# A state space stage cut into small pieces and its output units moved behind the last keys

## The chip, the cores and the metric

The kernel runs on one core of a Trainium2 chip. The metric is the device time of one execution in microseconds. Five engines matter: TensorE (PE in the profile; its weight loads are PEld), VectorE (DVE), ScalarE (ACT), GpSimd (POOL) and SyncE (SP), which issues DMAs. Each engine works through its own list of instructions strictly in order.

## The reference, cut to what matters

512 tokens of width 1024 pass through one block of a first kind and then through four layers of a second kind. The change touches the first block alone:

```
h = rmsnorm(x, norm_mix_g)
proj = h @ w_in                       # u (512 wide), q, k, v (512 each)
y_ssm = s5_mixer(u, ...)              # state space stage
y_att = chunked_attention(q, k, v, rel_bias)
mixed = concat(rmsnorm(y_ssm), rmsnorm(y_att))
x = x + mixed @ w_out
x = x + (silu(h2 @ w_gate) * (h2 @ w_up)) @ w_down    # h2 = rmsnorm(x)

# s5_mixer: 32 groups of 16 channels, 64 complex states per group
lam_bar = exp(lam * exp(log_dt))
b_bar   = ((lam_bar - 1) / lam) * b
state_t = lam_bar * state_{t-1} + b_bar @ u_t
y_t     = real(c @ state_t) + d_skip * u_t
y = gelu(y);  y = y * sigmoid(y @ w_glu + b_glu)
```

The attention has 8 heads of 64 channels; a token sees its own chunk of 64 tokens and the 8 chunks ahead of it. The four later layers also attend to a memory of 256 tokens, whose keys and values (`mem_n @ w_kv`) this kernel computes early, inside the first block's stretch.

## The kernel before

**Products.** Every large product is made in fp32 as three matmuls of a high and a low part (`mm`, L174; lines L185, L187, L189). A weight tile's high part is made by a ScalarE copy (L233), its low part by a VectorE subtraction (L235). The plan is a list of units; a unit is one output tile over four k-tiles, 12 matmuls of 128x512. I call these the main matmuls and count them from the start; those of the memory are 128x256.

**Order.** `execute` (L123) emits the units one after the other. Side work is written as generators. After each main matmul `tick(self.fine)` takes every generator of one list a step further, after each unit `tick(self.gens)` those of the other; `finish(g)` (L204) runs a generator to its end at once. `wait(n)` passes n ticks. A scheduler then moves instructions a little by readiness, and from there every engine's list is fixed.

**The first block before.** Main matmuls 0 to 96 are the four tiles of u. Their norm is gathered (L336) when `squares` (L1509) calls `finish` after the first 48. 96 to 480 are the memory's keys and values for four layers. 480 to 696 are q, k and v for head pairs 0 to 2, 696 to 744 the four output units of the state space stage (`ssm_units`, L1486; they read yh, yl, and SSM_AT = 3 puts them there), 744 to 816 q, k and v of pair 3, 816 to 1008 the two halves of w_out. Then the feed-forward part begins.

**The state space stage before.** `s5_tables` (L1100) makes powers of lam_bar and the matrices of b_bar in many small VectorE operations. `s5_u` (L1249) copies a tile of u out of PSUM, scales it by the norm's factors `bc` (L1257) and writes it to DRAM. `s5_main` (L1322) starts when the tables are done. It loads u per chunk of 8 tokens, makes the chunks' states by 64 small matmuls (S), and spawns `s5_toeps` (L1288), which makes the powers F of the output matrices (`s5_powers`, L1265: 12 operations of 288 elements per quarter m, L1278 to L1283), multiplies them into the kernels within a chunk (L1305), writes these to DRAM and reads them back as Toeplitz matrices `toep`. The recurrence over chunks is 14 steps of three dependent GpSimd operations: L1357 (product, 512 elements), L1358 (sum of the pair, 256), L1359 (added to S, 256). Then come four output stages, m = 0 to 3: S2 is copied out of S (L1370, GpSimd), 16 matmuls S,F (L1376) and 16 matmuls U,toep (L1384) go into one PSUM bank, the result y is copied to a buffer s5x (L1392) and sent to DRAM. F has two buffers, so F of m = 2 and 3 is made after the stages 0 and 1 have read theirs. `s5_gelu` (L1404) reads y back turned, applies gelu (L1415), and splits it into yh, yl.

**Attention.** `qkv_post` (L1572) scales q and makes keys (L1432), then spawns `chunk_pair` (L1437): scores, row maximum and exp (L788), scaling of the probabilities (L1451), transposes, and the product with v (L1469).

## Time and profile before

| | us |
|---|---|
| median of 3 runs (3158.51 to 3159.5) | 3159.09 |
| the profiled execution, its own time | 3160.28 |
| its span | 3158.5 |
| TensorE busy in the span | 3085.0 (98%) |
| VectorE busy | 1773.8 (56%) |
| ScalarE busy | 1362.7 (43%) |
| GpSimd busy | 561.1 (18%) |

TensorE is busy almost throughout, so the average says little. The page's strip of 40 slices shows where it is not: in the first four slices, of 79 us each, its digits are 7, 8, 9, 9, and VectorE's are 9, 9, 8, 7, while in most of the rest VectorE stands at 3 to 5. The first block takes about the first fifth of the span, and the stages that the change touches end where the feed-forward part begins, at 333.42 us. What matters is therefore read by stretches of that part. In the views below, a stretch is given in us from the span's start; PEclk is the granted TensorE clock as a share of full speed; L185, L187 and L189 on xh, xl or yh, yl are main matmuls.

### The profile page before, as it was taken

The numbers are of one execution on the slowest core, as the hardware profiler recorded it, in microseconds if no ns is written. First come the engines' busy times: TensorE is split into PE (matmuls) and PEld (weight loads), VectorE is DVE, ScalarE is ACT, GpSimd is POOL, SyncE is SP. The second block draws the span as 40 slices with busy tenths as digits, with TensorE's granted clock in tenths as the row PEclk, the third lists the DMA queues.
The fourth block names the chain that finished last, engine by engine and source line by source line (L and its number), as shares of the span: only waits on it lengthen the run. The fifth ranks groups of instructions, "written<-read, shape, count | busy, mean of one in ns | idle before, by whom it ended". The sixth has DMA issues, their size and how long they took to land.

```text
span 3158.5 us, 38988 instructions
## 1 busy us (share of the span) xinstructions
PE 3085.0 (98%) x14568; PEld 2576.1 (82%) x14568; DVE 1773.8 (56%) x2995; ACT 1362.7 (43%) x2504; POOL 561.1 (18%) x464
## 2 busy tenths in 40 slices
PE   7898999999999999999999999999999999999998
PEld 6687788888888888888888888887888888878886
DVE  9987644458755344467753445655444477553444
ACT  5366423347754232455432334334333477542332
POOL 2731201032212010111110001112000122120103
PEclk9899999999999999999999999999999999999999
DMA  6332233332223333322233333233333322233332
GB/s 211 110 99 87 85 96 97 98 94 68 69 73 104 100 91 103 94 77 84 67 103 98 92 103 91 86 102 99 96 96 98 98 67 67 62 106 97 94 101 77
DMA packets 101694, 295.28 MB, mean 93 GB/s; under 512 B 22496, under 2 KB 26592, under 8 KB 101472
## 3 DMA queue, kind: packets, MB, share of 16 engines
q1 hardware_dynamic: 101504, 292.79, 31.7%
q8 instruction: 114, 1.87, 0.2%
q14 instruction: 76, 0.62, 0.1%
HBM read 286.20 MB, written 6.55 MB: 93 GB/s over the span
## 4 chain that ended last, share of the span: by engine, by line
PE 91%; DVE 5%; ACT 1%; issue 1%; DMA 1%; POOL 0%; DVEq 0%; SPq 0%; ACTq 0%; POOLq 0%
PE g L185 27%; PE g L189 27%; PE g L187 27%; DVE lo L235 1%; PE a L225 1%; PE a L224 1%; PE z L740 1%; PE a L223 1%; PE z L753 1%; PE a L657 0%; PE a L646 0%; DVE x L427 0%; PE z L189 0%; PE z L185 0%; PE z L187 0%
## 5 line engine op out<-in xcount | busy, mean ns | idle before, releaser
L233 ACT ACTIVATE hi<-raw 128x512 fp32r<-128x512 f32 (+2 forms) x1094 | 662.2, 607 | 1419.3 <-PE g L187 1309.2
L235 DVE TENSOR_TENSOR lo<-raw,hi 128x512 fp32r<-128x512 f32 (+2 forms) x1094 | 765.3, 701 | 656.9 <-ACT hi L233 633.1
L185 PE MATMUL g<-xh,hi 128*128 128x512 f32 x2720 | 1066.6, 392 | 11.5 <-ACT hi L233 7.4
L189 PE MATMUL g<-xh,lo 128*128 128x512 f32 x2720 | 1064.0, 391 | 0.0
L187 PE MATMUL g<-xl,hi 128*128 128x512 f32 x2720 | 1062.6, 391 | 0.0
L185 PEld LDWEIGHTS g<-xh,hi 128*128 128x128 f32 x2720 | 513.0, 189 | 118.7 <-ACT hi L233 7.4
L189 PEld LDWEIGHTS g<-xh,lo 128*128 128x128 f32 x2720 | 512.3, 188 | 105.5 <-DVE lo L235 0.2
L187 PEld LDWEIGHTS g<-xl,hi 128*128 128x128 f32 x2720 | 512.7, 188 | 103.3
L189 PE MATMUL g<-ah,lo 128*128 128x512 f32 x1110 | 433.7, 391 | 3.0 <-DVE lo L235 2.8
L185 PE MATMUL g<-ah,hi 128*128 128x512 f32 x1110 | 432.2, 389 | 2.0 <-ACT t L284 2.0
L187 PE MATMUL g<-al,hi 128*128 128x512 f32 x1110 | 432.1, 389 | 0.0
L440 POOL TENSOR_TENSOR t<-t,bc 128x512 f32<-128x512 f32 x110 | 143.2, 1302 | 1407.3 <-ACT t L439 1407.3
L189 PEld LDWEIGHTS g<-ah,lo 128*128 128x128 f32 x1110 | 208.4, 188 | 50.7 <-DVE lo L235 7.8
L185 PEld LDWEIGHTS g<-ah,hi 128*128 128x128 f32 x1110 | 208.4, 188 | 45.3 <-ACT t L284 2.8
L187 PEld LDWEIGHTS g<-al,hi 128*128 128x128 f32 x1110 | 208.4, 188 | 43.1
L411 DVE TENSOR_TENSOR t<-g,bc 128x512 f32<-128x512 f32 x182 | 124.9, 688 | 169.2 <-PE g L189 164.0
L427 DVE TENSOR_TENSOR x<-x,g 128x512 f32<-128x512 f32 x151 | 103.3, 685 | 133.8 <-PE g L189 133.8
L442 DVE TENSOR_TENSOR t<-g,t 128x512 f32<-128x512 f32 x110 | 76.1, 692 | 180.4 <-PE g L189 160.6
L285 POOL TENSOR_TENSOR acc<-acc,t 128x512 f32<-128x512 f32 x82 | 114.9, 1405 | 329.9 <-ACT t L284 303.7
L233 ACT ACTIVATE ah<-t 128x512 fp32r<-128x512 f32 x110 | 69.5, 632 | 45.4 <-DVE t L442 45.4
L439 ACT ACTIVATE t<-t 128x512 f32<-128x512 f32 x110 | 69.7, 634 | 33.4 <-DVE t L411 33.3
L235 DVE TENSOR_TENSOR al<-t,ah 128x512 fp32r<-128x512 f32 x110 | 76.1, 692 | 11.9 <-ACT ah L233 2.3
(351 smaller groups left out, 3033.1 us busy)
## 6 DMA issues: line engine op xcount, KB each, us to landing
raw<-in_weights_dram SPq DMA_DIRECT2D x436, 512.0 KB, 3.6
raw<-in_weights_dram SPq DMA_DIRECT2D x76, 448.0 KB, 3.4
raw<-in_weights_dram SPq DMA_DIRECT2D x18, 384.0 KB, 3.2
x<-in_xT_dram SPq DMA_DIRECT2D x16, 256.0 KB, 3.7
x<-in_att_bias_dram SPq DMA_DIRECT2D x8, 256.0 KB, 6.2
kv<-kv SPq DMA_DIRECT2D x32, 64.0 KB, 2.4
out_dram<-x SPq DMA_DIRECT2D x8, 256.0 KB, 2.3
mraw<-in_memT_dram SPq DMA_DIRECT2D x2, 512.0 KB, 6.3
```

The source lines that it names most:

```text
L185: nc.tensor.matmul(out=out, lhsT=wh, rhs=xh, start=u.first and i == 0, stop=False)
L187: nc.tensor.matmul(out=out, lhsT=wh, rhs=xl, start=False, stop=False)
L189: nc.tensor.matmul(out=out, lhsT=wl, rhs=xh, start=False, stop=u.last and i == len(u.ks) - 1)
L223: nc.tensor.matmul(out=out, lhsT=ah, rhs=bh, start=start, stop=False)
L233: nc.scalar.activation(out=hi, in_=src, func=ACTF.Copy)
L235: eng.tensor_tensor(out=lo, in0=src, in1=hi.bitcast(F32), op=ALU.subtract)
L285: nc.gpsimd.tensor_tensor(out=norm["acc"][rows, :n], in0=norm["acc"][rows, :n], in1=sq[rows, :n], op=ALU.add)
L411: nc.vector.tensor_tensor(out=t, in0=ps, in1=bc, op=ALU.mult)
L427: self.nc.vector.tensor_tensor(out=self.x[m], in0=self.x[m], in1=ps, op=ALU.add)
L439: nc.scalar.activation(out=tg, in_=tg, func=ACTF.Silu)
L440: nc.gpsimd.tensor_tensor(out=tg, in0=tg, in1=self.bc(n), op=ALU.mult)
L442: nc.vector.tensor_tensor(out=h, in0=ps, in1=tg, op=ALU.mult)
```

## The change

- The tables are cut into small pieces, with a `yield` after every few operations, and `finish` on the first norm goes. `s5_u` copies u out of PSUM at once, into a free tile of x, and waits as a generator until `bc` is there before it scales and stores ("u scaled late").
- `s5_powers` makes F of a quarter in 6 operations of 576 elements, all on VectorE, 6 ticks apart (S5_PACE).
- A new generator `s5_kernels` makes F and the kernels within a chunk before `s5_main` starts. `s5_toeps` only clears the matrices, on GpSimd now, and reads the kernels from DRAM; it stands after the state matmuls.
- `s5_main` waits until all four tiles of u and the kernels are done. The recurrence's 42 operations move from GpSimd to VectorE.
- F for m = 2 and 3 is made after y of m = 0 and 1 has been sent off.
- The four output units move from ahead of q3 to between k3 and v3, and with them `ssm_begin`, which finishes `s5_main`. The attention of a pair waits for its v.

```diff
@@ -52,12 +52,11 @@
-S5_STEP = 10
-S5_FILL = (24, 0)
-S5_POOL = (False, True)
-S5_WAIT = 100
+S5_STEP = 14
+S5_FILL = 8
+S5_PACE = 6
+S5_WAIT = 4
-SSM_AT = 3
...
+        def cmul(out_r, out_i, xr, xi, yr, yi, t, eng, pace=False):
             eng.tensor_tensor(out=out_r, in0=xr, in1=yr, op=mul)
             eng.tensor_tensor(out=t, in0=xi, in1=yi, op=mul)
+            if pace:
+                yield
...
-            cmul(pw[:, 0, :, lo + 1:lo + 1 + w], pw[:, 1, :, lo + 1:lo + 1 + w],
-                 pw[:, 0, :, 1:1 + w], pw[:, 1, :, 1:1 + w], b[0], b[1], t[:, :, :w], V)
+            yield from cmul(pw[:, 0, :, lo + 1:lo + 1 + w], pw[:, 1, :, lo + 1:lo + 1 + w],
+                            pw[:, 0, :, 1:1 + w], pw[:, 1, :, 1:1 + w], b[0], b[1], t[:, :, :w], V)
+            yield
         bb = tail[:, :512].rearrange("p (c a b) -> p c a b", c=2, a=16)
-        cmul(bb[:, 0], bb[:, 1], br, bi, w3[0], w3[1], t, V)
+        yield from cmul(bb[:, 0], bb[:, 1], br, bi, w3[0], w3[1], t, V, True)
+        yield
+        V.tensor_scalar(out=ci, in0=ci, scalar1=-1.0, scalar2=None, op0=mul)
...
@@ -1249,11 +1269,14 @@
     def s5_u(self, m, ps, norm):
-        t = self.tmp()
+
+        t = self.x[4 + m]
         turned = t.rearrange("p (t c) -> p c t", t=8)
         src = ps.rearrange("p (c t) -> p c t", t=8)
 
         nc.scalar.activation(out=turned, in_=src, func=ACTF.Copy)
+        while norm["bc"] is None:
+            yield
         nc.vector.tensor_tensor(
...
-    def s5_powers(self, m, split=(False, False)):
+    def s5_powers(self, m, store, key):
+
+        V = self.nc.vector
...
-        F = self.s5.tile([P, 2, 4, 9, 16], F32, tag="big", name="F", bufs=2)
-        for q in range(2):
-            js, ls = slice(4 * m + 2 * q, 4 * m + 2 * q + 2), slice(2 * q, 2 * q + 2)
-            G = nc.gpsimd if split[q] else nc.vector
-            t = (self.s5_tmp() if q else self.tmp())[:, :288]
-            t = t.rearrange("p (a b c) -> p a b c", a=2, b=9)
-            G.tensor_tensor(out=F[:, 0, ls], in0=x[0], in1=y[0], op=ALU.mult)
-            G.tensor_tensor(out=F[:, 0, ls], in0=F[:, 0, ls], in1=t, op=ALU.subtract)
...
-    def s5_toeps(self):
+        F = store[key] = self.s5.tile([P, 2, 4, 9, 16], F32, tag="big", name="F", bufs=2)
+        js, shape = slice(4 * m, 4 * m + 4), [P, 4, 9, 16]
+        x = [v[:, js].unsqueeze(2).to_broadcast(shape) for v in (cr, ci)]
+        y = [self.s5_pw[:, c, js].unsqueeze(3).to_broadcast(shape) for c in range(2)]
+        t = self.s5_tmp().rearrange("p (a b c) -> p a b c", a=4, b=9)
+        for c, op in ((0, ALU.add), (1, ALU.subtract)):
+            V.tensor_tensor(out=F[:, c], in0=x[c], in1=y[0], op=ALU.mult)
+            yield from wait(S5_PACE)
+            V.tensor_tensor(out=t, in0=x[1 - c], in1=y[1], op=ALU.mult)
+            yield from wait(S5_PACE)
+            V.tensor_tensor(out=F[:, c], in0=F[:, c], in1=t, op=op)
+            yield from wait(S5_PACE)
+    def s5_kernels(self, before):
         nc, pool = self.nc, self.s5
+        while before in self.gens:
+            yield
         for pair in (1, 0):
-            toep = self.toep[pair] = pool.tile([P, 8, 2, P], F32, tag="tab", name="toep", bufs=2)
-            nc.vector.memset(toep, 0.0)
-            k_dram = self.k_dram[pair]
-                F = self.powers[2 * pair + m] = self.s5_powers(2 * pair + m)
-                yield from wait(S5_FILL[0])
+                yield from self.s5_powers(2 * pair + m, self.powers, 2 * pair + m)
+                F = self.powers[2 * pair + m]
+                yield from wait(S5_FILL)
...
+    def s5_toeps(self):
+
+        nc = self.nc
+        for pair in (0, 1):
+            toep = self.toep[pair] = self.s5.tile([P, 8, 2, P], F32, tag="tab", name="toep", bufs=2)
+            nc.gpsimd.memset(toep, 0.0)
-    def s5_main(self, tables):
-        nc = self.nc
-        while tables in self.gens:
+    def s5_main(self, before):
+        nc = self.nc
+        while any(g in self.gens or g in self.fine for g in before):
             yield
...
-        self.toep, self.powers = {}, {}
-        toeps = self.spawn(self.s5_toeps(), self.fine)
+        self.s5_toeps()
...
-            G.tensor_tensor(out=pr, in0=src.to_broadcast(shape), in1=fac, op=ALU.mult)
-            G.tensor_tensor(out=pr[:, :, 0:16], in0=pr[:, :, 0:16], in1=pr[:, :, 16:32], op=ALU.add)
-            G.tensor_tensor(out=dst, in0=dst, in1=pr[:, :, 0:16], op=ALU.add)
+            V.tensor_tensor(out=pr, in0=src.to_broadcast(shape), in1=fac, op=ALU.mult)
+            V.tensor_tensor(out=pr[:, :, 0:16], in0=pr[:, :, 0:16], in1=pr[:, :, 16:32], op=ALU.add)
+            V.tensor_tensor(out=dst, in0=dst, in1=pr[:, :, 0:16], op=ALU.add)
             yield from wait(S5_STEP)
-        while toeps in self.fine:
-            yield
...
-            if m < 2:
-                self.powers[m + 2] = self.s5_powers(m + 2, S5_POOL)
-            y = self.s5_tmp()
             nc.sync.dma_start(out=self.y_dram[m].rearrange("p g c -> p (g c)"), in_=y)
+            if m < 2:
+                yield from self.s5_powers(m + 2, self.powers, m + 2)
             yield
...
             yield from wait(PAIR_GAPS[2])
+            while "v" not in st:
+                yield
...
             self.begin_norm(st["norm"], D, 1e-6, gap=0)
-            self.finish(st["norm"]["gen"])
...
             st["tables"] = self.spawn(self.s5_tables())
+            self.toep, self.powers = {}, {}
+            st["kernels"] = self.spawn(self.s5_kernels(st["tables"]), self.fine)
         def u_post(m, ps):
-            self.s5_u(m, ps, st["norm"])
+            st["u", m] = self.spawn(self.s5_u(m, ps, st["norm"]))
+            next(st["u", m], None)
             if m == 3:
-                st["s5"] = self.spawn(self.s5_main(st["tables"]), self.fine)
+                before = [st["u", k] for k in range(4)] + [st["kernels"]]
+                st["s5"] = self.spawn(self.s5_main(before), self.fine)
...
         for j in range(4):
-            if j == SSM_AT:
+            outs = [
+                Out(self.xg, "w_in.0", 4 + 4 * i + j, lambda ps, i=i, j=j: qkv_post(j, i, ps))
+                for i in range(3)
+            ]
+            self.units(outs[:2], HALVES)
+            if j == 3:
                 self.ssm_units(ssm_begin, glu_post)
-            self.units(
-                [
-                    Out(self.xg, "w_in.0", 4 + 4 * i + j, lambda ps, i=i, j=j: qkv_post(j, i, ps))
-                    for i in range(3)
-                ], HALVES,
-            )
-        if SSM_AT == 4:
-            self.ssm_units(ssm_begin, glu_post)
+            self.units(outs[2:], HALVES)
```

**TensorE, at the first gather of the norm.** In before, L336 gathers the norm right after main matmul 48 (xh_107 is the last of eight k-tiles):

```order
L187 MATMUL g<-xl_115,hi 128x512
L189 MATMUL g<-xh_107,lo 128x512
L302 MATMUL a<-ones,t 128x2 x4
L336 MATMUL a<-t,minus 128x512
L185 MATMUL g<-xh_100,hi 128x512
```

and in after main matmuls follow at once:

```order
L186 MATMUL g<-xl_115,hi 128x512
L188 MATMUL g<-xh_107,lo 128x512
L301 MATMUL a<-ones,t 128x2 x4
L184 MATMUL g<-xh_100,hi 128x512
L186 MATMUL g<-xl_108,hi 128x512
L188 MATMUL g<-xh_100,lo 128x512
```

The gather (now L335) has moved behind 34 to 36 main matmuls of the second half of u.

**TensorE, at the output stages of the state space stage.** S,F and U,toep are the output matmuls, a<-ident are attention's transposes, kh,q its scores, th,vs and tl,vs its products with v. In before the last stage stands between main matmuls of pair 2:

```order
L218 MATMUL a<-kh,q 128x256
L219 MATMUL a<-kl,q 128x256
L189 MATMUL g<-xh_107,lo 128x512
L1376 MATMUL s5ps<-S_1338,F 128x128 x2
L1384 MATMUL s5ps<-U,toep 128x64 x2
```

In after the last main matmul of k3, and what follows it, is

```order
L186 MATMUL g<-xl_115,hi 128x512
L805 MATMUL a<-ident,p 128x128 x2
L188 MATMUL g<-xh_107,lo 128x512
L217 MATMUL a<-kh,q 128x512
L218 MATMUL a<-kl,q 128x512
L217 MATMUL a<-kh,q 128x384
```

and the list reaches the next main matmul, the first of the output units, only here, at the end of the fourth stage:

```order
L1397 MATMUL s5ps<-S_2417,F 128x128 x2
L1405 MATMUL s5ps<-U,toep 128x64 x2
L184 MATMUL g<-yh_2539,hi 128x512 x3
L186 MATMUL g<-yl_2540,hi 128x512
L188 MATMUL g<-yh_2539,lo 128x512
```

The 64 state matmuls, the last scores and all four output stages now lie between these two places, with no main matmul among them.

**GpSimd and VectorE, the recurrence.** In before GpSimd has the steps one behind the other:

```order
L1357 TENSOR_TENSOR pr<-S,s5p 128x512
L1358 TENSOR_TENSOR pr<-pr 128x2x128
L1359 TENSOR_TENSOR S<-S,pr 128x32x8
L1357 TENSOR_TENSOR pr<-S,s5p 128x512
```

In after VectorE has them, and behind the last step the operations of F for m = 2 and 3 (L1299 to L1303) and the low parts of y (yl):

```order
L1380 TENSOR_TENSOR pr<-S,s5p 128x512
L1381 TENSOR_TENSOR pr<-pr 128x2x128
L1382 TENSOR_TENSOR S<-S,pr 128x32x8
L1299 TENSOR_TENSOR F<-s5p,s5t_615 128x576 x2
L1301 TENSOR_TENSOR s5x<-s5p,s5t_615 128x576
L1303 TENSOR_TENSOR F<-F,s5x 128x576
```

Ahead of the recurrence VectorE's list holds all key work of pair 3 (L1453), and no weight's low part stands between that and the first yl.

## Rows read from the trace of the kernel before

**Rows 1.** Windows: stretch, length; busy PE, PEld, DVE, ACT, POOL; PEclk, DMA, GB/s.

```profile
0.00:50.00 50.00, 30.39 (x123) 24.46 (x124) 43.17 (x140) 28.84 (x50) 15.27 (x16) 0.90 0.63 216
76.00:133.00 57.00, 41.92 (x396) 38.09 (x396) 56.21 (x65) 18.61 (x32) 49.04 (x40) 0.90 0.34 99
133.00:227.00 94.00, 89.83 (x501) 75.82 (x501) 78.47 (x157) 54.22 (x114) 34.74 (x36) 0.97 0.43 114
227.00:334.00 107.00, 96.28 (x430) 78.47 (x431) 84.75 (x152) 66.45 (x124) 22.77 (x17) 0.92 0.24 72
62.00:75.00 13.00, 13.00 (x111) 13.00 (x110) 11.99 (x24) 6.64 (x11) 3.60 (x3) 1.00 0.75 240
400.00:425.00 25.00, 25.00 (x112) 20.70 (x111) 10.94 (x17) 8.64 (x14) 2.58 (x2) 1.00 0.30 97
```

**Rows 2.** Timeline, TensorE: start, length; memory's end, first output unit, feed-forward part.

```profile
133.15 0.77 PE L185 MATMUL g<-xh,hi 128*128 128x512 f32 x1
...
227.38 1.65 PE L185 MATMUL g<-yh,hi 128*128 128x512 f32 x3 [3.21 <-ACT yh L233]
...
333.42 0.39 PE L185 MATMUL g<-xh,hi 128*128 128x512 f32 x1
```

**Rows 3.** Waits, TensorE, 0 to 334 us: who waits for whom; us, count, longest.

```profile
PE a L336 <- DVE t L322: 15.8, 3, 6.6
```

**Rows 4.** Groups by form, VectorE, 76 to 133 us: count, busy us, mean ns.

```profile
L235 DVE TENSOR_TENSOR lo<-raw,hi 128x512 fp32r<-128x512 f32 x17 | 18.9, 1128 | 0.0
...
L1278 DVE TENSOR_TENSOR F<-s5p,s5t 128x288 f32<-128x288 f32 x8 | 10.4, 1294 | 0.0
```

**Rows 5.** Groups by form, VectorE, 133 to 334 us.

```profile
L235 DVE TENSOR_TENSOR tl<-a,th 128x512 fp32r<-128x512 f32 x16 | 10.8, 685 | 3.2 <-ACT th L233 3.1
...
L235 DVE TENSOR_TENSOR tl<-a,th 128x256 fp32r<-128x256 f32 x8 | 3.3, 412 | 0.0
...
L788 DVE CUSTOM_DVE_ANT_0 p<-a,x 128x384 f32<-128x384 f32 x8 | 4.4, 551 | 0.0
...
L1451 DVE TENSOR_SCALAR p<-p,sm 128x384 f32<-128x384 f32 x8 | 5.2, 644 | 0.0
...
L1432 DVE TENSOR_TENSOR kl<-t,kh 64x512 fp32r<-64x512 f32 x8 | 9.8, 1222 | 0.9 <-ACT kh L1431 0.8
```

**Rows 6.** Groups by form, GpSimd, 0 to 334 us: the recurrence and the copies S2.

```profile
L1357 POOL TENSOR_TENSOR pr<-S,s5p 128x512 f32<-128x512 f32 x14 | 20.7, 1482 | 6.0 <-ACT S L1343 5.0
L1359 POOL TENSOR_TENSOR S<-S,pr 128x256 f32<-128x256 f32 x14 | 14.6, 1044 | 0.9
L1358 POOL TENSOR_TENSOR pr<-pr 128x256 f32<-128x256 f32 x14 | 13.9, 992 | 1.1
...
L1370 POOL COPY S<-S 64x512 f32<-64x512 f32 x8 | 5.7, 717 | 0.3
```

**Rows 7.** Timeline, TensorE: first and last group of one output stage.

```profile
170.00 0.61 PE L1376 MATMUL s5ps<-S,F 128*128 128x128 f32 x4
...
173.12 0.56 PE L1384 MATMUL s5ps<-U,toep 128*128 128x64 f32 x4
```

**Rows 8.** Line L1257, scaling of u with turned axes: least, mean, most ns.

```profile
L1257 DVE TENSOR_TENSOR t<-t,bc x4: 1041/1064/1089, 39.0 to 52.3; 128x512 f32<-128x512 f32 x4
```

**Rows 9.** Chain of waits: start, length; from the last y to yh.

```profile
218.32 0.60 ACT s5x L1392
218.94 2.01 DMA y_dram<-s5x
221.09 3.05 DMA t<-y_dram
224.31 1.28 ACT L1415
225.60 1.07 ACT y L1415
```

**Rows 10.** Windows, as rows 1, ahead of the memory norm's gather.

```profile
42.00:51.00 9.00, 2.35 (x11) 1.83 (x10) 8.86 (x31) 2.45 (x3) 3.79 (x3) 0.75 0.38 95
```

More of the change, by code (lines that the diff above doesn't have):

```diff
@@ L1097, in s5_tmp @@
     def s5_tmp(self):
-        return self.s5.tile([P, T], F32, tag="s5x", name="s5x")
+        return self.s5.tile([P, 576], F32, tag="s5x", name="s5x")
     def s5_tables(self):
@@ L1175, in s5_tables @@
         V.reciprocal(out=rec, in_=den)
+        yield
         wr = tt(tt(tt(ar, lr, mul), tt(ai, li, mul), add), rec, mul)
+        yield
         wi = tt(tt(tt(ai, lr, mul), tt(ar, li, mul), sub), rec, mul)
+        yield
         pw = keep(2, 16, 9)
@@ L1218, in s5_tables @@
             b = [L[:, c, 0, :, w - 1:w].to_broadcast([P, 16, w]) for c in (0, 1)]
-            cmul(L[:, 0, 0, :, w:2 * w], L[:, 1, 0, :, w:2 * w], L[:, 0, 0, :, :w], L[:, 1, 0, :, :w],
-                 b[0], b[1], t[:, :, :w], V)
+            yield from cmul(L[:, 0, 0, :, w:2 * w], L[:, 1, 0, :, w:2 * w], L[:, 0, 0, :, :w],
+                            L[:, 1, 0, :, :w], b[0], b[1], t[:, :, :w], V)
+            yield
         V.tensor_scalar(out=L[:, 0, 1], in0=L[:, 1, 0], scalar1=-1.0, scalar2=None, op0=mul)
@@ L1232, in s5_tables @@
             y = [pv[:, c, js].unsqueeze(3).to_broadcast([P, 4, 8, 16]) for c in range(2)]
-            t = (self.s5_tmp() if m % 2 else self.tmp()).rearrange("p (a b c) -> p a b c", a=4, b=8)
-            cmul(A[:, 0], A[:, 1], x[0], x[1], y[0], y[1], t, G if m % 2 else V)
+            t = (self.s5_tmp()[:, :T] if m % 2 else self.tmp()).rearrange("p (a b c) -> p a b c", a=4, b=8)
+            yield from cmul(A[:, 0], A[:, 1], x[0], x[1], y[0], y[1], t, G if m % 2 else V, m % 2 == 0)
             yield
@@ L1263, in s5_u @@
         )
-    def s5_powers(self, m, split=(False, False)):
-        nc = self.nc
+    def s5_powers(self, m, store, key):
+        V = self.nc.vector
         cr, ci = self.s5_c
-        F = self.s5.tile([P, 2, 4, 9, 16], F32, tag="big", name="F", bufs=2)
-        for q in range(2):
-            js, ls = slice(4 * m + 2 * q, 4 * m + 2 * q + 2), slice(2 * q, 2 * q + 2)
-            shape = [P, 2, 9, 16]
-            x = [v[:, js].unsqueeze(2).to_broadcast(shape) for v in (cr, ci)]
-            y = [self.s5_pw[:, c, js].unsqueeze(3).to_broadcast(shape) for c in range(2)]
-            G = nc.gpsimd if split[q] else nc.vector
-            t = (self.s5_tmp() if q else self.tmp())[:, :288]
-            t = t.rearrange("p (a b c) -> p a b c", a=2, b=9)
-            G.tensor_tensor(out=F[:, 0, ls], in0=x[0], in1=y[0], op=ALU.mult)
-            G.tensor_tensor(out=t, in0=x[1], in1=y[1], op=ALU.mult)
-            G.tensor_tensor(out=F[:, 0, ls], in0=F[:, 0, ls], in1=t, op=ALU.subtract)
-            G.tensor_tensor(out=F[:, 1, ls], in0=x[0], in1=y[1], op=ALU.mult)
-            G.tensor_tensor(out=t, in0=x[1], in1=y[0], op=ALU.mult)
-            nc.vector.scalar_tensor_tensor(
-                out=F[:, 1, ls], in0=F[:, 1, ls], scalar=-1.0, in1=t, op0=ALU.mult, op1=ALU.subtract
-            )
-        return F
@@ L1313, in s5_toeps @@
                 for q in range(2):
-                    nc.sync.dma_start(out=k_dram[:, 4 * m:4 * m + 4, q], in_=kt[16 * q:16 * q + 16])
-                yield from wait(S5_FILL[1])
+                    nc.sync.dma_start(out=self.k_dram[pair][:, 4 * m:4 * m + 4, q], in_=kt[16 * q:16 * q + 16])
+    def s5_toeps(self):
[3 more added lines that the diff above has]
+            nc.gpsimd.memset(toep, 0.0)
             for t in range(8):
@@ L1318, in s5_toeps @@
                     out=toep[16 * t:16 * t + 16, :, :, 16 * t:P].rearrange("p j q c -> p (j q) c"),
[L1319 removed]
+                    in_=self.k_dram[pair].rearrange("h j q c -> h (j q) c")[:, :, 0:P - 16 * t],
                 )
[L1322 removed]
+    def s5_main(self, before):
         nc = self.nc
[L1324 removed]
+        while any(g in self.gens or g in self.fine for g in before):
             yield
```

20 lines of the change are left out of this document (15 added, 5 removed).

## The prediction

> **What bounds the kernel now.** I read the windows first, since the page's average (TensorE 98%) hides the stages. In steady work TensorE is all there is: in 400 to 425 us it is busy 25.00 of 25.00 us with 112 matmuls of 512 columns, 0.223 us each, and 13.00 us hold 111 of the memory's 256 columns, 0.117 us each [rows 1]. So a span can only shrink where TensorE stands idle, and up to 334 us it does so in three places: 0 to 50 (busy 30.39), 76 to 133 (41.92 of 57) and 227 to 334 (96.28 of 107) [rows 1]. The timeline gives the milestones: the memory's products end at 133.15, the first output unit starts at 227.38, the feed-forward part at 333.42 [rows 2]. From there on the two kernels' lists are the same, so the change is worth what it does to 333.42, and the rest keeps its length.
>
> Who holds TensorE up? In the first stretch the waits name the norms' gathers, 15.8 us in 3 waits for VectorE's spread [rows 3], and VectorE is busy 43.17 of 50 us. In 76 to 133 VectorE is busy 56.21 of 57 us [rows 1]: it is the bound there, TensorE is not. Its operations are also long: the weights' low parts take 1128 ns [rows 4], where an operation of the same 512 columns takes 685 ns later [rows 5], and in this stretch GpSimd is busy too, 49.04 us, mostly with the recurrence [rows 1, 6]. From 133 to 227 TensorE is the bound, 89.83 of 94 [rows 1]. The state space stage runs hidden behind this: its recurrence, on GpSimd, is 14 steps of 1.48 + 0.99 + 1.04 = 3.5 us [rows 6], done long before 227, and an output stage, 3.68 us from 170.00 to 173.12 + 0.56 [rows 7], fills a hole between main matmuls. Only the last y is late: 3.21 us of idle ahead of the first output unit [rows 2].
>
> **The change part by part.** I build the new times of five points: M, the memory's end (133.15 before); K, where VectorE has done pair 3's keys; R, the end of the recurrence; G, the first output unit; F, the feed-forward part (333.42 before).
>
> *M: the front.* Removed from TensorE's way up to here are the stall at the first gather, VectorE's making of F, and the recurrence beside it. I give the first 76 us only 1 us, since VectorE was busy nearly throughout them and keeps the same work (the tables still precede the kernels); if the gathers' stalls went with nothing behind them, it would be some 8 us. After 76 VectorE's list up to the last memory product holds 17 low parts (0.685 each), 8 memory results of 256 columns (0.41 each) and 5 table operations of 512: some 20 us where there were 56.21. TensorE then is the bound: 192 products by 0.117 = 22.5 us and the tables' transposes, some 3. M = 75 + 25.5 = 101 (92 to 108). That is 32 us gained.
>
> *K: where the gain goes.* What was taken out of 76 to 133 comes back behind M. Between M and pair 3's keys VectorE's list now has 71 operations of 512 columns by 0.685 [rows 5] = 48.6; 24 of F, 576 columns each, by 0.685 x 576/512 = 0.77: 18.5; five heads' row maxima (pieces under 512 columns, 0.55 for 384 of them, some 1.5 a head) and scalings (0.64 for 384 columns, some 2.0 for a head's 1280) [rows 5]: 17; sixteen small ones by 0.41 = 6.6; the keys' low halves at 1.22 instead of 0.685 [rows 5], eight times 0.54 = 4.3; and some 2 of waits for the kernels' small DMAs. Sum 97 (89 to 102). TensorE has 264 main matmuls there, 59 us, and with attention some 87, so VectorE is the bound. K = 101 + 97 = 198 (184 to 206).
>
> *R: the recurrence on VectorE.* It cannot start earlier: `s5_main` waits for kernels that end near main matmul 712, and `ssm_begin` behind k3 finishes it. A step is a product of 512 and two sums of 256. The trace has them only on GpSimd (3.5 us, upper bound 49 us for 14); by VectorE's 0.685 and twice 0.412 [rows 5] a step is 1.51 and 14 are 21.1 (lower bound). The first seven steps walk S with a stride of 8 elements; the row nearest to that is the scaling of u with turned axes, 1064 ns instead of 685 [rows 8], 1.55 times, which makes the 14 steps 21.1 + 7 x 1.51 x 0.55 = 26.9 if all three operations suffer and some 25 if not all; I take 24. Beside them in the same list stands the attention of pairs 2 and 3, some 20 us by the same rows. R = 198 + 44 = 242 (226 to 252).
>
> [...]
>
> *G: the output stages, uncovered.* Behind k3's last product TensorE's list has no main matmul until the fourth output stage is through. This is the heart of it: what was hidden before now has nothing to hide it. In order: the copies S2, two by 0.72 [rows 6], and stage 0, 3.68 [rows 7]: 5.1 us. y goes through the single buffer s5x, 0.60 and a DMA of 2.01 [rows 9]; the temporary of F is that same buffer, so F of m = 2 (6 x 0.77, of which one can go ahead) ends near 11.6; stage 1 runs beside it. y of stage 1 needs the buffer back, 0.6 + 2.0, and F of m = 3 ends near 18; stage 3 near 21.7. Then the last y: copy 0.60, DMA 2.01, back 3.05, table load 1.28, gelu 1.07, split 0.7 [rows 9], in all 9.1 from the last product to 227.38 [rows 2]. G = R + 31 = 273 (28 if the stages overlap better; the clock is a rival, below).
>
> *F: the rest.* Before, G to F took 106 us for 312 main matmuls (69.6) and 36.4 of attention, of the wait for y and of the norm of the attention. Now it is 264 by 0.223 = 58.9; the gelus of the other three k-tiles, of which a part is waited for, 4; the output norm and the attention norm, with the last pair's product with v, 13 (16.7 was before between the last product and w_out's main stretch). F = 273 + 76 = 349 (G + 72 to G + 80).
>
> The profiled execution has 3160.28 us, 1.19 over the median. F moves from 333.42 to 349, 16 us later: 3176 for such an execution, **3175** for the median. VectorE's and GpSimd's other edits are at no cost: the matrices' clearing goes to a GpSimd that no longer has the recurrence; the Toeplitz DMAs stand on SyncE behind the state matmuls and run beside the recurrence's 44 us, and the raw weights queued behind them are needed only after G. If that cover went, the first output unit would have its weights some 4 us late. The four scalings of u, moved late, cost VectorE what they cost before.
>
> **The rivals.** *A, the forecast*: 3166 to 3188, by K to F above.
>
> [...]
>
> *C, the other side: VectorE is freed for good.* If the long operations of 76 to 133 are long because of GpSimd (1128 against 685 [rows 4, 5]), then with the recurrence off GpSimd everything on VectorE up to K may run at its short durations, the key halves and the gathers' stalls too: M = 92, K = 92 + 90 = 182, and with the lower bounds R = 224, G = 252, F = 324: 9 us earlier than before, 3150. It decides if K comes before about 183 us (333.4 - 76 - 31 - 44). Against: I have already priced K's work at the short durations.
>
> *D, the pieces do not help the front.* If the tables, cut up and ticked once per unit, end later, so that TensorE's transposes for them hold up the memory's products, M is about 115 and everything after it 14 later: 3189.
>
> *E, nearly nothing.* Gains and losses cancel, with M near 95, R + 28 and G + 73: 3153 to 3166.
>
> **How the numbers follow.** A 0.55, B 0.18, D 0.06, E 0.12, C 0.09. A measurement of this kernel can tell about 0.2%, 6.3 us, from no change, so "same" is 3152.8 to 3165.4. Faster takes C, 0.09; same takes E and a little of A's low end, 0.14; slower the rest, 0.77. The range leaves out C and what lies beyond B and D: 3153 to 3194.
>
> **What would show it.** Right: L1380 to L1382 on VectorE between some 200 and 245 us, a TensorE idle for most of 205 to 270, the first output unit near 273 behind a wait for yh, the memory's end near 101, VectorE as the bound between. Wrong: a recurrence that ends before 225 (K too high, or attention off its list), a first output unit less than 25 us behind it (F made beside the stages), or a memory's end after 110. [...]

## The result, and the profile after

The changed kernel takes 3197.09 us (median of 4 runs, 3196.33 to 3197.38), before 3159.3 beside it: ratio 1.0119, 95% interval 1.0101 to 1.0136. It is slower, as forecast, but by 38 us where 16 were forecast, and outside the range.

Timeline of TensorE in after, at the milestones of [rows 2] (start, length, in brackets the idle time ahead and its releaser): the memory's end, the first output matmuls of the state space stage, the first output unit, the feed-forward part.

```profile
97.33 0.47 PE L184 MATMUL g<-xh,hi 128*128 128x512 f32 x1
...
249.29 1.22 PE L1397 MATMUL s5ps<-S,F 128*128 128x128 f32 x4 [26.80 <-POOL S L1391]
...
285.45 1.65 PE L184 MATMUL g<-yh,hi 128*128 128x512 f32 x3 [9.45 <-ACT yh L232]
...
367.52 0.39 PE L184 MATMUL g<-xh,hi 128*128 128x512 f32 x1
```

The memory's end is 36 us earlier than in [rows 2], the first output unit 58 us later, the feed-forward part 34 us later. The windows (columns as in rows 1) show where:

```profile
97.00:190.00 93.00, 93.00 (x453) 68.91 (x453) 74.90 (x156) 53.05 (x113) 11.90 (x9) 1.00 0.29 86
...
236.00:249.00 13.00, 0.00 (x0) 0.00 (x0) 11.18 (x22) 0.00 (x0) 0.97 (x2) 0.50 0.00 0
249.00:276.00 27.00, 21.78 (x128) 21.24 (x128) 9.74 (x12) 1.79 (x3) 5.77 (x7) 0.73 0.08 30
276.00:286.00 10.00, 0.56 (x2) 0.50 (x2) 0.51 (x1) 4.17 (x5) 0.00 (x0) 0.73 0.64 131
```

From 97 to 190 TensorE works without a gap (93.00 of 93.00 us). Then main matmuls stop (k3's last stands at 190.77) and the rest of the chain is laid bare: recurrence, output stages at a granted clock of 0.73, and the way of y. (In after's trace the granted clock has two values alone: 0.50, as from 248 to 252, here the lower level, and 1.00, as from 272 to 280, the upper; a mean between them is a stretch with both.) The chain's own milestones are read from two lines' groups (least, median, most ns; first and last start): the kernels within a chunk and the states.

```profile
L1323 PE MATMUL s5ps<-F,bd x64: 272/273/297, 114.5 to 182.3; 128*32 128x128 f32 x64
...
L1361 PE MATMUL a<-U,Ain x128: 222/222/369, 194.9 to 208.6; 128*64 128x64 f32 x128
```

In before the states were made at 84.3 to 90.1. The next table has all runs, in us, each but the time from its trace: M the memory's end, then the first state matmul, the recurrence and its engine (V VectorE, G GpSimd), the end of the last output stage, G the first output unit, F the feed-forward part. The variants are single runs but for scaleact, wmixd5 and wmixq. Before's own runs spread from 3156.9 to 3162.7, so a difference below some 4 us between two single runs tells nothing.

| run | M | states | recurrence | stages end | G | F | time |
|---|---|---|---|---|---|---|---|
| before | 133.2 | 84.3 | G 90.9 to 162.6 | 218.3 | 227.4 | 333.4 | 3159.3 |
| after | 97.3 | 194.9 | V 209.5 to 247.9 | 276.0 | 285.5 | 367.5 | 3197.1 |
| short | 97.1 | 194.7 | V 209.4 to 236.7 | 262.5 | 272.0 | 353.8 | 3181.8 |
| clock | 97.2 | 194.8 | V 210.2 to 249.1 | 273.8 | 287.3 | 369.2 | 3198.0 |
| late | 97.6 | 199.4 | V 210.3 to 252.5 | 280.3 | 290.1 | 370.7 | 3199.4 |
| pool | 97.4 | 194.9 | G 210.5 to 257.6 | 285.6 | 295.0 | 377.2 | 3205.3 |
| front_only | 134.6 | 91.6 | G 99.6 to 167.6 | 219.9 | 229.0 | 334.9 | 3161.7 |
| place | 133.8 | 84.9 | G 91.5 to 163.3 | 218.9 | 237.0 | 335.9 | 3163.8 |
| recdve | 117.7 | 85.7 | V 99.8 to 182.9 | 233.0 | 242.3 | 344.4 | 3172.6 |
| recplace | 117.8 | 85.3 | V 99.5 to 182.9 | 238.5 | 247.7 | 332.0 | 3161.0 |
| fast | 97.4 | 128.8 | V 154.7 to 234.3 | 263.6 | 272.8 | 356.4 | 3185.5 |
| mixd | 96.6 | 103.8 | V 131.0 to 228.7 | 261.6 | 271.0 | 353.0 | 3181.3 |
| mixp | 97.5 | 104.6 | G 132.1 to 193.6 | 250.2 | 259.7 | 341.4 | 3169.4 |
| tabwhole | 128.8 | 99.8 | V 122.0 to 186.9 | 241.0 | 255.0 | 337.5 | 3165.2 |
| wfast | 118.0 | 87.5 | V 99.1 to 175.9 | 217.0 | 230.8 | 331.0 | 3158.8 |
| wmixd | 115.9 | 86.7 | V 94.2 to 168.6 | 211.2 | 223.4 | 320.3 | 3148.6 |
| wmixp | 124.4 | 87.1 | G 95.5 to 156.9 | 200.9 | 235.7 | 335.1 | 3162.6 |
| wmixd5 | 116.3 | 86.1 | V 94.5 to 169.0 | 211.7 | 223.8 | 321.6 | 3148.4 |
| wmixq | 115.3 | 86.2 | V 93.5 to 168.0 | 207.1 | 219.0 | 322.1 | 3150.5 |
| scaleact | 133.8 | 84.9 | G 91.5 to 164.1 | 218.2 | 229.9 | 348.4 | 3174.9 |

### The profile page after: what moved, and what is told of

Its sections match the earlier page's. It is cut to its first block, busy times and chain, and to the rows that moved or that the text cites. A ratio compares the mean times of both kernels' runs of the same rounds, so it can differ in the third digit from the quotient of the medians.

```text
span 3194.6 us, 38946 instructions
## 1 busy us (share of the span) xinstructions
PE 3098.3 (97%) x14568; PEld 2578.7 (81%) x14568; DVE 1764.1 (55%) x3010; ACT 1360.1 (43%) x2502; POOL 509.7 (16%) x414
## 4 chain that ended last, share of the span: by engine, by line
PE 91%; DVE 6%; ACT 1%; issue 1%; DMA 1%; POOL 0%; SPq 0%; DVEq 0%; ACTq 0%; POOLq 0%
PE g L184 27%; PE g L188 27%; PE g L186 27%; DVE lo L234 1%; PE a L224 1%; PE a L223 1%; PE z L739 1%; PE a L222 1%; DVE x L426 1%; PE z L752 1%; PE a L656 0%; PE a L301 0%; PE a L645 0%; PE s5ps L1397 0%; PE a L671 0%
```

## The experiments

**Is the bare chain the bound?** short takes away half of the recurrence:

```diff
-        for i in range(14):
+        for i in range(7):
```

> After, with the last seven of the recurrence's 14 steps left out (the states are then carried within groups of eight chunks only). These took 236.4 to 247.9 us, 11.5 us. If the chain recurrence, output stages, y is what TensorE waits for, all behind it moves by 11 to 12 us, and the time falls to 3184 to 3187. If the keys, the attention or the weights would be late next anyway, it falls by less than 5.

F came 13.7 us earlier and the time fell by 15, more than the 11 to 12 expected. The chain is what TensorE waits for: the recurrence ends 11.2 us earlier, and the stages behind it came out 2 us shorter.

**The clock.** clock keeps TensorE busy with spare matmuls (in each of the last seven steps, and after the last stage):

```diff
+                for k in range(5):
+                    nc.tensor.matmul(
...
+                        rhs=inner[:, 0, :, i - 6, :], start=i == 7 and k == 0, stop=i == 13 and k == 4,
+                    )
...
+        for k in range(7):
+            nc.tensor.matmul(out=spare, lhsT=self.ident, rhs=y, start=k == 0, stop=k == 6)
```

> After, with spare matmuls whose result nobody reads: 5 of 128 columns behind each of the last seven steps of the recurrence, and 7 of 512 behind the last output stage, so that TensorE is not idle ahead of the stages and of the output units. Theory 2 (clock): the first two stages take 3.6 us instead of 5.5 and 6.7, the last output matmul ends some 6 us earlier, the first output units run at 0.22 us a product: time 7 to 10 us less than after. Theory 1 alone (single buffers and copies set the stages' pace): the stages get shorter but wait longer for the copies of S and for F, and the time falls by 0 to 3 us.

In the trace of clock the same stretches read:

```profile
236.00:250.00 14.00, 10.64 (x67) 10.44 (x68) 12.27 (x24) 0.00 (x0) 0.82 (x2) 0.69 0.01 1
250.00:274.00 24.00, 18.92 (x133) 18.18 (x131) 9.74 (x12) 1.93 (x4) 5.94 (x7) 0.86 0.09 34
```

The four stages took 3.8, 5.4, 5.4 and 3.8 us, in after 5.7, 6.9, 5.4 and 3.8: 3.4 us less, of which 2.2 reached the end of the last stage, since the recurrence ended 1.2 us later. The spare matmuls on y then held its way up (13.6 us from the last stage to G instead of 9.4), so the whole gained nothing, and neither theory's figure can be read from it.

The clock's whole price in the stages is larger than the 3.4 us that the run took away. In after the groups of four matmuls S,F take 1.17 to 1.22 us all through the second stage and 0.66 to 0.71 all through the fourth, at a granted clock of 0.53 (257 to 264) and of 1.00 (271 to 276.1), and within a stage TensorE has no gap (timeline of TensorE; first groups of the second and the fourth stage):

```profile
256.99 1.22 PE L1397 MATMUL s5ps<-S,F 128*128 128x128 f32 x4 [2.01 <-POOL S L1391]
...
272.22 0.71 PE L1397 MATMUL s5ps<-S,F 128*128 128x128 f32 x4 [1.07 <-POOL S L1391]
```

In before all four stages took 3.68, at 1.00. So the 7.1 us by which after's stages, 21.8 us together, exceed 4 x 3.68 are the lower level's; in clock the groups S,F of the second and third stage rose from 0.66 to 1.17 us half-way. Behind G the first twelve main matmuls of after start 0.43 us apart, at 0.50 (285.4 to 290.7), and the later ones 0.23, at 1.00 (293 to 300): some 2 us more.

**The place of the output units.** late puts them behind v3 in after (its edit is shown); place makes the change's own move, between k3 and v3, alone in before:

```diff
-            self.units(outs[:2], HALVES)
-            if j == 3:
-                self.ssm_units(ssm_begin, glu_post)
-            self.units(outs[2:], HALVES)
+            self.units(outs, HALVES)
+        self.ssm_units(ssm_begin, glu_post)
```

> After, with the four output units behind v3 instead of ahead of it. Theory 1 (the hole on TensorE is set by the chain keys, recurrence, output stages, y; whatever stands beside it is free): the first output unit stays at about 285 us (283 to 290), and the 24 products of v3 (5.4 us) and pair 3's product with v, which stood behind it, now lie in the hole; the feed-forward part starts at 355 to 360 instead of 367.5, the time falls by 8 to 12 us. Theory 2 (the lower clock in and behind the hole is what cost more than forecast): as much, and a little more, since the hole is shorter. Rival (VectorE's work for v3 pushes the recurrence back): the output units move to about 293, and the time is as in after.

> Before, with the output units between k3 and v3 and nothing else (the attention of a pair waits for its v). Here the state space stage is through by 227 us, so the units should find yh ready near 240 and no hole opens ahead of them. What the place costs by itself is behind them: the norm of their result takes some 15 us from the last unit to w_out, and only v3 is left to cover it, where q3, k3 and v3 were. Expected: the feed-forward part at 333 to 342 instead of 333.4, time 0 to 8 us more. If the place itself were what made after slow, it would be 20 us or more.

late missed its figure, and its rival took it (G at 290.1, the time as in after). VectorE's work for v3 pushed the recurrence's end from 247.9 to 252.5, and what v3 no longer covered opened behind the units, a second hole, while the norm of their result is made (timeline of late):

```profile
311.72 1.86 PE L301 MATMUL a<-ones,acc 128*128 128x2 f32 x8 [6.29 <-POOL acc L284]
```

place held: F is 2.5 us later, and the time 4 us above before's beside it. The place alone is not what costs 38 us.

**The front alone**, in before (no `finish` in `squares`, u scaled late):

```diff
-            self.finish(st["norm"]["gen"])
...
-        t = self.tmp()
+        t = self.x[4 + m]
...
+        while norm["bc"] is None:
+            yield
```

> Before, with the front edit alone: u is copied out at once and scaled late, and the first norm is not finished at once; tables, kernels, recurrence on GpSimd and output units as in before. If the 36 us that after gains up to the memory's end came from the gathers' stalls, they come here too: the memory's end at 97 to 115 instead of 133. If they came from VectorE's work moved away from there (my reading), it stays at 125 to 133, and the time falls by 0 to 6 us.

M stayed at 134.6, though up to 120 us the waits of L336 fell from 12.2 to 4.5 us. (The third wait of [rows 3], 3.5 us, stands at 313 us, ahead of w_out.) The edit alone is worth nothing: behind the stalls TensorE meets VectorE's other work (there it waits 6.1 us for F and 7.1 for `kvt`).

**The recurrence's engine.** pool moves it back to GpSimd in after, recdve to VectorE in before, recplace adds the units' new place to recdve (the first of the three operations, in pool):

```diff
-            V.tensor_tensor(out=pr, in0=src.to_broadcast(shape), in1=fac, op=ALU.mult)
...
+            G.tensor_tensor(out=pr, in0=src.to_broadcast(shape), in1=fac, op=ALU.mult)
...
```

> After, with the recurrence's 42 operations back on GpSimd, nothing else. Theory 1: the recurrence still starts at about 210, when the states are there; on GpSimd it takes 14 x 3.5 = 49 us and the clearing of the matrices stands ahead of it, so it ends at 260 to 264 instead of 248, and everything behind it is 12 to 16 us later: span 3207 to 3211. Rival (moving the recurrence to VectorE is what cost the time, since it shares VectorE with attention): it ends no later than 248, and the time falls by 5 to 20 us.

> Before, with the recurrence's 42 operations on VectorE, nothing else. If GpSimd's work beside it is what lengthens VectorE's operations, the weights' low parts in 76 to 133 us take some 690 ns on the mean instead of 1128, and F's operations 450 instead of 1294. VectorE gains 21 to 25 us of recurrence there and loses some 18 of lengthening, so the memory's end comes at 133 to 141. If the lengthening has another cause, the low parts stay near 1100 and the memory's end comes at 150 to 158.

> Before, with the recurrence on VectorE and the output units between k3 and v3. With the recurrence on VectorE alone the last output matmul came at 233 and the output units at 242, with q3 and k3 behind them; now these lie in front. If a hole ahead of the units is what cost the 11.6 us there, 48 products and pair 3's scores (some 15 us) fill it, and the time falls by 5 to 12 us against that run, to 3161 to 3168. If VectorE's total work is what cost them, it stays within 3 us of 3172.6.

pool ended the recurrence 9.7 us later and F with it, less than the 12 to 16 expected: laid bare, VectorE is the better engine. In recdve the low parts of 76 to 133 us got shorter, between the two expectations (groups of VectorE, to be held against [rows 4]):

```profile
L235 DVE TENSOR_TENSOR lo<-raw,hi 128x512 fp32r<-128x512 f32 x23 | 18.3, 807 | 0.0
...
L1278 DVE TENSOR_TENSOR F<-s5p,s5t 128x288 f32<-128x288 f32 x8 | 5.8, 721 | 0.0
```

1128 became 807 ns, 1294 became 721, with GpSimd busy 10.71 of 57 us where it was 49.04 [rows 1]. So GpSimd's work does lengthen these operations of VectorE, and the memory's end came 15.5 us earlier, though VectorE had the recurrence besides: earlier than either expectation. But G came 15 us later, and the time rose by 11.6. recplace, which lets q3 and k3 lie ahead of the units, took this back to 3161.0, within the spread of before. Recurrence on VectorE and units in their new place together cost nothing that can be told from noise, and neither does the late scaling of u (front_only). What is left is F in six operations, the pacing, the cut tables and the kernels' place, and all but the first bear on where the chain starts.

**What starts it late.** fast sets the pieces closer (S5_PACE 1, S5_FILL 2, S5_STEP 5, S5_COPIED, the ticks ahead of a stage, 3 in after); mixd makes the states ahead of the kernels (pieces 2, 4, 5, 4), mixp has the recurrence on GpSimd besides (pieces 2, 4, 8, 4); of mixd's edit:

```diff
-        self.s5_toeps()
+        kernels = self.spawn(self.s5_kernels(None), self.fine)
...
+        while kernels in self.fine:
+            yield
+        self.s5_toeps()
...
```

> After, with the pieces closer together: a tick between F's operations instead of 6, 2 instead of 8 ahead of the kernels' matmuls, 5 instead of 14 between the recurrence's steps, 3 instead of 8 ahead of a stage. The states then stand near main matmul 570 to 600 instead of 744. Theory 1 (the chain starts too late): the recurrence is through at 215 to 228 instead of 248, VectorE's total work being the bound, the first output unit comes at 252 to 265, and the time falls by 20 to 33 us. Rival (VectorE's total work alone sets the end): the recurrence pushes the keys back by its own length, and the time falls by less than 10.

> After, with the states right behind the tables (near main matmul 505 to 554), then the recurrence on VectorE with F and the kernels made beside it, the pieces closer together (1 to 5 ticks), output units still between k3 and v3. Theory 1 (a chain that starts too late, behind the kernels): the recurrence ends at 200 to 220 instead of 248, the output units come at 235 to 255 instead of 285, and the time falls by 30 to 45 us, to 3152 to 3167. Rival (VectorE's total work sets the end, whatever the order): the keys come later by what comes earlier, and the time falls by 10 to 15, as for the closer pieces alone.

> As the last one, with the recurrence on GpSimd. Theory 1: GpSimd has from about 125 to 180 for it, off VectorE; VectorE's operations are longer beside it, some 10 to 15 us in all; output units at 225 to 250, time 3147 to 3165. Rival (VectorE's lengthening beside GpSimd costs more than the recurrence itself): output units later than in the run with the recurrence on VectorE, time above it by 3 us or more.

fast and mixd gained 12 and 16 us, less than theory 1 asked and just above the rivals' figures (less than 10, and 10 to 15). The recurrence starts 55 and 78 us earlier than in after, but ends only 14 and 19 us earlier, since it now stands in VectorE's list between attention and the weights, and that list is full (window of fast, VectorE 79.04 of 80 us):

```profile
155.00:235.00 80.00, 62.66 (x289) 48.93 (x288) 79.04 (x157) 40.92 (x92) 16.12 (x12) 0.88 0.30 75
```

mixp beat mixd by 12 us: beside this full VectorE, GpSimd is the better engine, though it lengthens VectorE's work here too (a weight's low part takes 1085 ns in 134 to 195 us, 757 in mixd). Theory 1's figure was missed, and the rival, that the lengthening costs more than the recurrence, fell.

Then the tables were made in a few long pieces again (before's `s5_tables`, with ci negated), in after (tabwhole), in fast (wfast), mixd (wmixd) and mixp (wmixp).

> After, with the tables made in a few long pieces as in before, all else as in after (kernels ahead of the states, recurrence on VectorE, output units between k3 and v3). If the cutting of the tables into pieces, one a unit, is what starts the chain late, the states come 90 us earlier than the 195 of after, the memory's end moves back to 110 to 125, and the output units come at 235 to 255 instead of 285: time 3155 to 3172. If it is the kernels' place ahead of the states, the output units stay above 270 and the time above 3182.

> The last one, with the later pieces closer together too (1, 2, 5 and 3 ticks). If the chain still has slack against VectorE's other work, the output units come another 5 to 10 us earlier, at 230 to 245, time 3150 to 3165; if VectorE is full, no change to the last one within 3 us.

> The last one, with the states ahead of the kernels as in before. The recurrence then starts at about 95 and the kernels are made beside it. Expected output units at 235 to 248 and a time of 3150 to 3163, near before with the recurrence on VectorE and the output units moved (3161); more than 3170 if the order of kernels and states matters by itself.

> The last one, with the recurrence on GpSimd: before's own arrangement with u scaled late, F in six long operations and the output units between k3 and v3. Expected as before with the output units moved, 3157 to 3166; the states' chain is hidden, the memory's end is back at 125 to 135 since GpSimd lengthens VectorE's operations there.

On one chip, with before at 3157.5, tabwhole took 3165.2, wfast 3158.8 and wmixd 3148.6. tabwhole came as expected of the cutting: its states come 95 us earlier and G at 255.0, though M, 128.8, lies above its 110 to 125. Held against before beside each, after loses 37.8 us and tabwhole 7.7, so the cut tables alone are some 30 of the 38 us. Closer pieces bring 6.5 more and the step to wmixd 10, which puts it below the 3150 to 3163 expected. These two sizes hold for this order of steps: with the tables still cut they were 12 (fast) and 16 (mixd). The 10 us are not simply the kernels' place either. In wfast the scheduler has already put the states (87.5 to 96.5) ahead of most of the kernels' matmuls (92.1 to 150.1), and the pieces differ too; what they come from is not shown.

The kernels' matmuls in tabwhole (in after they stand at 114.5 to 182.3, above), the tables' matmuls in before and in after, and the states in tabwhole show how the cut tables do it:

```profile
L1303 PE MATMUL s5ps<-F,bd x64: 272/273/297, 92.0 to 141.4; 128*32 128x128 f32 x64
```

```profile
L1242 PE MATMUL a<-ident,A x32: 270/272/329, 57.4 to 86.5; 128*128 128x128 f32 x32
```

```profile
L1262 PE MATMUL a<-ident,A x32: 270/272/273, 84.2 to 100.9; 128*128 128x128 f32 x32
```

```profile
L1341 PE MATMUL a<-U,Ain x128: 222/246/270, 99.8 to 120.4; 128*64 128x64 f32 x128
```

The tables themselves end only 14 us later in after (100.9 instead of 86.5). But each piece is a step of the list taken once per unit, so the generator ends near main matmul 492 (336 in before, 355 in tabwhole). The kernels start counting their ticks there, among products of 512 columns and attention, and end at 182, main matmul 712, instead of 141. The states stand in the code behind the kernels, and in after in TensorE's list too. In tabwhole the scheduler has moved them in among the kernels' matmuls; why it does so there and not in after was not tried.

The early memory's end goes with the late chain. With whole tables M falls back from 97.3 to 128.8, and VectorE is not the reason (busy 34.32 of 53 us in 76 to 129): the 128 state matmuls and 48 of the 64 of the kernels now stand ahead of M on TensorE, busy 46.82. What the change gains at M and what it loses behind K have for the most part one cause, the stage's place behind the memory. A part of the gain can be had with an early chain: in recdve and wmixd, with the recurrence on VectorE, M comes at 117.7 and 115.9.

wmixp fell back to before's level, as expected: there GpSimd's recurrence lengthens VectorE's work again (a low part takes 1212 ns in 76 to 134 us, in wmixd 784), and M comes at 124.4 instead of 115.9. Here the lengthening decides, since TensorE waits for the lengthened operations (6.0 us up to M for `kvt` and F, in wmixd not at all) and not for the chain: the last stage is through at 200.9, and G comes at 235.7.

**A version that beats both.** wmixd5 is wmixd again, in five runs; wmixq has the units between q3 and k3:

```diff
-            self.units(outs[:2], HALVES)
+            self.units(outs[:1], HALVES)
...
-            self.units(outs[2:], HALVES)
+            self.units(outs[1:], HALVES)
```

scaleact moves the probabilities' scaling in before to ScalarE, because VectorE is so full:

```diff
-                nc.vector.tensor_scalar(
-                    out=p[:, c], in0=p[:, c], scalar1=sm[:, i:i + 1], scalar2=None, op0=ALU.mult
-                )
+                nc.scalar.activation(out=p[:, c], in_=p[:, c], func=ACTF.Copy, scale=sm[:, i:i + 1])
```

> The best of the last four again (tables whole, pieces close together, states ahead of the kernels, recurrence on VectorE, output units between k3 and v3), now timed. Expected 3148 (3146 to 3151), a ratio to before of 0.995 to 0.998, one that excludes 1.

> The same, with the output units between q3 and k3, so that k3 and v3 stand behind them. In the last trace TensorE is idle for most of 250 to 270, where the norm of the output units' result is made and v3 is used up; k3's 24 products and pair 3's scores would lie there. If the fourth stage is through by then, the time falls by 2 to 6 us, to 3143 to 3147; if the chain is late instead, a hole opens ahead of the units and it rises by 3 to 8.

> Before, with the 32 scalings of the probabilities (L1451, 16 us in all on VectorE) on ScalarE, nothing else. In all orders tried VectorE is the engine that is nearly full up to the feed-forward part, and ScalarE is not (196 of 334 us). If VectorE's total work bounds the stretch, the time falls by 3 to 10 us; if the order of the chain alone does, by 0 to 2; if ScalarE's splits of the weights get late by it, it rises.

wmixd5 took 3148.42 (5 runs), as expected: the ratio to before is 0.9965, the interval 0.9952 to 0.9977. wmixq took 3150.45 (7 runs), 0.9969 (0.9957 to 0.9980), and is no better: G came 4.8 us earlier and F did not. scaleact rose to 3174.9 (4 runs, ratio 1.0046, 1.0029 to 1.0062): off VectorE is not off the path. From 133 us to the feed-forward part ScalarE got 15.3 us of scaling and 11 table loads of 1.28 us where there were 5. None of the loads stands at a scaling: 6 stand at exp (3 in before), 2 at gelu (1) and 3 at the sigmoid (1). Whether the scaling or the loads cost more was not tried. In wmixd TensorE is busy 101.40 and VectorE 96.79 of the 107 us from 116 to 223, up to the first output unit.

## Why the prediction was right and wrong

- **M**: 101 us were forecast and 97.3 measured. The sums behind 76 us were right: only the tables and the memory's own work stand ahead of M there, on either engine. The rest came ahead of 76 us, where the forecast gave 1 us: 152 of the memory's products were left behind it, not 192. front_only shows that the stalls at the gathers were not the cause, and tabwhole that 31 of the 36 us gained go again when the stage comes early.
- **K**: 198 forecast, and pair 3's last key operation on VectorE ends at 198.4. That the number fits is luck. From 97 to 190 VectorE was busy 74.90 of 93 us and TensorE 93.00: TensorE was the bound, with 93 us where the forecast gave it 87, and the 4 us gained at M were lost again here.
- **R**: 242 forecast, 247.9 measured. The recurrence's steps were sized well (groups of VectorE in after):

```profile
L1380 DVE TENSOR_TENSOR pr<-S,s5p 128x512 f32<-128x512 f32 x14 | 12.6, 899 | 0.6 <-ACT S L1367 0.3
...
L1382 DVE TENSOR_TENSOR S<-S,pr 128x256 f32<-128x256 f32 x14 | 7.8, 555 | 0.3
...
L1381 DVE TENSOR_TENSOR pr<-pr 128x256 f32<-128x256 f32 x14 | 6.0, 426 | 0.4
```

  Their sum is 26.4 us, where the forecast took 24 out of 21.1 to 26.9. In the first seven steps, which walk S with the stride, the two operations on S take 1106 and 686 ns on the mean, in the last seven 692 and 424; the sum of the pair, whose operands are contiguous, stays at 427. So two of the three suffer, 1.6 times each. With the attention beside them VectorE had 44.09 us of work from K to R, and the forecast's 44 was right (window of VectorE in after):

```profile
198.43:247.90 49.47, 16.60 (x154) 12.73 (x154) 44.09 (x96) 17.74 (x44) 8.35 (x5) 0.68 0.18 40
```

  What failed is the start, which the forecast put at K. The states were not there until 208.9: their matmuls start only at 194.9, behind k3's last product, and take 14.0 us among the last attention's (5.9 in before). VectorE idled 4.3 of the 11 us up to the recurrence, 5.4 up to R.
- **G**: 31 us behind R forecast, 37.6 measured. The forecast priced every stage at the 3.68 of [rows 7]; the four took 21.8 us, 7.1 more, and this is the lower clock, which stands among the chances as B. The upper end of the forecast's range, 3194, counts on all four stages wholly at that clock, and no run shows such a term: in after the second stage ran so but for its last group (6.9 us), the first and the third in part (5.7 and 5.4), the fourth not at all (3.8). The rest of the path was another one, of nearly the same length by luck. The forecast had F's making on it; F's making ran beside the stages. In its place stand the copies S2: the buffer is one, so each copy waits for the stage before and takes 1.27 to 2.22 us, between the stages (timeline of GpSimd in after):

```profile
247.97 1.27 POOL L1391 COPY S<-S 64x512 f32<-64x512 f32 x2 [24.36 <-DVE S L1382]
254.72 2.22 POOL L1391 COPY S<-S 64x512 f32<-64x512 f32 x2 [5.48 <-PE s5ps L1397]
```

  Four stages of 3.68 and the 6.3 us between them would make 21.0 us (an estimate from these rows), where the forecast had 21.7 and 28.1 were measured. The way of y was right, 9.4 us for 9.1.
- **F**: 76 us behind G forecast, 82.0 measured. Some 2 us of the excess are the first twelve main matmuls at the lower clock. The output units' norm was counted as part of 13 us; late shows that it opens a hole of its own, 6.29 us, when nothing is left to cover it. How the other 4 us divide was not tried.
- So the step that failed is the sum behind K, with three terms too small: 5.5 us from K to R, where the recurrence was let start at K and its states were late; 6.6 from R to G, where the stages were priced at the upper clock; and 6.0 from G to F. With 0.4 at K they are the 18.5 us by which F, 367.5, came later than the 349 forecast. The mechanism, a chain laid bare behind k3, was right, as short shows. The clock, B, which the forecast's sum does not hold, came on top of it with these 7.1 us. 2 us more lie behind F (2827.1 us of span instead of 2825.1), where the rest was to keep its length; they were not explained, and other variants, wmixd with 2826.6 too, show some of it. The last 1.6 of the 22 us are the profiled executions, which lie on either side of their medians.
- What the text said of the cause was too narrow: "It cannot start earlier: `s5_main` waits for kernels". The kernels do end near main matmul 712, as forecast, but they are late because the tables, cut into one piece a unit, hand over late. Of the rivals, C was wrong: with a VectorE freed of GpSimd's company the front did gain, but the chain's place behind it decided. D was wrong too: the tables did end later, and M came early all the same.

## What to carry to other kernels

When side work is fed in by ticks, a generator's place is set by the steps that it takes, not by its work: cutting a producer into small pieces can delay the whole chain behind it far more than the pieces themselves take, and its consumers' pace should be counted from when their input is there. A gain ahead of the critical chain is only kept if that chain starts as early as before; read the start of the chain in the new order first, then the gain. Whether the recurrence belonged on GpSimd or VectorE turned with what TensorE waited for there. Laid bare, it belonged on the faster engine (VectorE in after, through at 247.9; GpSimd in pool, 257.6). Beside a full VectorE, GpSimd was better where the recurrence's own chain was waited for (mixp 3169.4, mixd 3181.3), and worse where TensorE waited for the operations that it lengthened (wmixp 3162.6, wmixd 3148.6).

## What was not expected of the hardware

The lengthening goes both ways. Two copies S2 on GpSimd took 1.27 us together alone and 2.22 us while VectorE made F; the recurrence's product on GpSimd took 1482 ns in before [rows 6], beside a VectorE busy 64.67 of 71.70 us, and 1292 ns in pool, where VectorE had less to do (an estimate: the 37.2 us that it is busy from 209.5 to 247.9 in after without the recurrence's 26.4, some 11). And work that leaves a busy VectorE for GpSimd isn't free: with GpSimd busy 49.04 of 57 us a weight's low part took 1128 ns [rows 4], at 10.71 of 57 us 807, and 688 in before's 400 to 600 us, where GpSimd is busy 13.51 of 200.

Not every operation of VectorE is lengthened. In mixp, with GpSimd busy 52.78 of 61 us, two operations of the same 512 columns stand beside each other (groups of VectorE, 134 to 195 us):

```profile
L234 DVE TENSOR_TENSOR lo<-raw,hi 128x512 fp32r<-128x512 f32 x10 | 10.8, 1085 | 0.1
...
L234 DVE TENSOR_TENSOR tl<-a,th 128x512 fp32r<-128x512 f32 x5 | 3.3, 677 | 0.0
```

raw and hi lie in SBUF, a in PSUM. The memory's results `kvt<-g,membc`, whose g lies in PSUM, are not lengthened either: 256 columns took 409 ns beside the 1128 ns of [rows 4], and 408 in recdve beside the 807. So the 685 ns of [rows 5], which the prediction set against the 1128, is a row of the kind that keeps its length; as the unlengthened price of a low part it came out right (688).
